# Four couples of delta heads, ScalarE statistics for three output tiles, and a smaller first constant

## The chip, the core and the metric

The kernel runs on one core of a Trainium2 chip. The core has TensorE (PE, matrix products into psum), VectorE (DVE), ScalarE (ACT), GpSimd (POOL) and SyncE (SP, which issues DMAs), each with its own queue of instructions, executed in order, and 16 DMA engines. The engines meet at semaphores. The metric is the device time of one execution in microseconds (us). The profile's span is the part of it between the first and the last recorded instruction.

## The reference

One step of a one-layer decoder, for one prompt of 512 tokens and 8 samples of 4 tokens, 544 tokens of width 1024 together:

```python
shift, scale, gate = split(silu(c) @ w_cond + b_cond)
h = x * (1 + scale) + shift
[qa, ka, va, za, qkv_b, zb, a_b, b_b, g_a, g_b] = h @ w_in     # 1024 x 11280
o_a = dilated window attention, 3 groups (128,1) (512,4) (2048,16), 8 heads x 64
o_b = gated DeltaNet, 8 heads x 128: conv of width 4, silu, l2norm, chunked delta rule
merged = sigmoid(g_a) * ((o_a * silu(za)) @ w_branch_a) + sigmoid(g_b) * ((norm(o_b) * silu(zb)) @ w_branch_b)
y = LayerNorm(ALPHA * x + gate * (merged @ w_out))
```

Beside y it returns the key and value caches (moved on by four rows), the convolution states and the delta states. The delta rule of a head treats the tokens in chunks of 64. Each chunk needs a unit lower triangular system solved:

```python
lower = where(strict, beta[:, None] * kk * decay, 0) + eye(n)
sol = triangular_solve(lower, concat([beta * v, beta * k * exp(cum)]))
```

and then the states pass from chunk to chunk. The last step, the LayerNorm over 1024 columns, needs a mean and a variance of every row.

## The kernel before

The weights of w_in come as 88 tiles of 1024 x 128. Each is loaded (wt), split by ScalarE and VectorE into a high part (hi) and the rest (lo), and multiplied with the tokens' high and low parts (hhi, hlo) in three products per 128 rows, two halves of 272 tokens each; the psum tiles are called pp. These 4080 matmuls are most of PE's work. The tiles are jobs in a list (`jobs`, from L2150), run in the list's order by `stream` (L1041): three convolution jobs (q, k, v) per delta head, nine attention jobs per pair of heads j, then za, zb and the gates. `conv_job` (L1219) of head h may begin only when head h - 3 is freed, which its `states` sets at its end, because KQ has three buffers.

Beside the stream run threads: `delta_blocks` (L1285) computes a head's decays and then the inverses of 16 x 16 blocks by substitution, fifteen pairs of VectorE instructions (tmp, then Tb) on 32 rows per head; `delta_rule` (L1389) joins the blocks to the inverse of a 64 x 64 system in six PE stages, two each at block size 16, 32 and 64 (`pd<-Tc,NTs`, `pd<-W,Xc`; `pd<-Tc,NTs`, `pd<-XF,W`; `pd<-U,NTs`, `pd<-XF,U`), with copies and transposes between them on ScalarE, VectorE and GpSimd; and `states` (L1471) carries the states through the four pairs of chunks, head after head. TOGETHER (L42) says which heads take substitution and stages in common: a couple's rows lie behind one another in the same tiles, so an instruction treats 64 rows, and a PE stage holds twice the matmuls. Before, heads 0 and 7 are alone and 1 to 6 form three couples. Other threads do the prompt's attention (`prompt_attention`), the samples' caches, and `sample_prep` (L1704), which takes the norms of the samples' queries and keys (kq: a square root on ScalarE, a reciprocal on VectorE) after head 7's convolutions.

No instruction goes to the chip as it is called. A `Recorder` keeps them with their dependencies, and its `schedule` (L459) plans the order of every engine's queue with a table of costs, by rank and readiness; `emit` (L708) issues them, at L727. Every row of the profile therefore names L727, and groups are told apart by tile names. A matmul on a part of the array (32x32, 64x64, 128x32) changes PE's form; the planner puts such a change off if it can.

The front (from L897) computes the conditioning. SP issues in order: cT, the first weights wc of part 1, bT, the constants cst, then xT, W (the 400 columns of the first projection) and wc in turn, then wc of part 0 and the first weight tiles. The constants are one table of identity, selectors (selc, selg), low16 and dmask. selc turns the conditioning rows into columns (`to_features`, L864), so it is needed at once; the identity is used by later transposes.

The end (from L2311) computes merged @ w_out by token tiles: r0 to r3 of 128 tokens by 1024 columns and r4 for the samples. VectorE scales the product by gate, adds the scaled input xr (scaled by ScalarE), takes bn_stats of each half, aggregates them to mean and variance (mv), and `norm_out` (L2332) ends with a square root on ScalarE and the normalisation on VectorE.

Of the kernel before, what the change touches and what calls it, by code (L numbers as in the profile page):

```python
# [11 lines left out]
F32 = mybir.dt.float32  # L12
# [7 lines left out]
D = 1024  # L20
# [18 lines left out]
GATES = (110.0, 200.0)  # L39
EARLY_A, EARLY_B = 7, 4  # L40
S0B = 7
TOGETHER = ((0,), (1, 2), (3, 4), (5, 6), (7,))  # L42
IDLE = (8, 2, 5)
CHUNKS = ((0, 1), (1, 1), (2, 2), (4, 2), (6, 2))

# [33 lines left out]
def shape_constants():  # L79

    p = np.arange(128)
    b4, i4, h8 = p // 32, p // 8 % 4, p % 8
    blk = {}
    blk["ident"] = np.eye(128)
    blk["selc"] = (p[:, None] % 32 == np.arange(9)[None, :])
    tok = np.arange(2 * NS)
    blk["selg"] = (p[:, None] % 32 == 1 + tok[None, :] % NS // 4)
    blk["triu"] = (p[:, None] <= p[None, :])
    same = p[:, None] // 4 == p[None, :] // 4
    blk["btri"] = same & (p[:, None] <= p[None, :])  # L90
    blk["bones"] = same
    blk["low16"] = np.where(p[:, None] % 32 >= 16, -1.0, 0.0)
    blk["strict4"] = same & (p[:, None] < p[None, :])
    blk["dmask"] = np.where(p[:, None] <= p[None, :], 0.0, -BIG)
    blk["dmask_s"] = np.where(same & (p[:, None] <= p[None, :]), 0.0, -BIG)
    blk["bmask"] = (p[:, None] % 32 // 4 == np.arange(8)[None, :])
    blk["quarter"] = np.where(p[:, None] % 32 == p[None, :] % 32, 0.25, 0.0)
    blk["hmask"] = (p[:, None] % 4 == np.arange(4)[None, :])
    sab = np.zeros((128, 4, 4))
    for h4 in range(4):  # L100
        for g in range(2):
            sab[4 * g + h4::16, h4, g] = 1.0
            sab[8 + 4 * g + h4::16, h4, 2 + g] = 1.0
    blk["selab"] = sab.reshape(128, 16)
    blk["sel16"] = p[:, None] % 16 == np.arange(16)[None, :]
    cols, blobs = {}, []
    for names in (("ident", "selc", "selg", "low16", "dmask"), ("selab", "sel16", "triu", "btri", "bones"),
                  ("strict4", "dmask_s", "bmask"), ("hmask",), ("quarter",)):
        at = 0
        for name in names:  # L110
            cols[name] = (at, blk[name].shape[1])
            at += blk[name].shape[1]
        blobs.append(np.ascontiguousarray(np.concatenate([blk[n] for n in names], axis=1), dtype=np.float32))
    return cols, blobs
# [665 lines left out]
def body(ctx, tc, io):  # L780
# [31 lines left out]
        return psp.tile([128, 512], F32, name="pp", tag="pp")  # L812


    cst = consts.tile([128, CONST[0].shape[1]], F32, name="cst")
    tables = {"early": cst}

    def take(gen, n):
        for _ in range(n):
# [44 lines left out]
    def to_features(pv, k, rows):  # L864

        for i in range(4):
            pe.matmul(pv[:, k + i, 0:9], rows[:, 128 * i:128 * i + 128], C("selc"), start=True, stop=True)

    f16 = lambda t: t[:, :128].rearrange("p (a b) -> p a b", b=16)

# [15 lines left out]
    n = CONST[1].shape[1]  # L886
# [8 lines left out]
    with ExitStack() as fctx:  # L895
# [35 lines left out]
        def cond_block(part, at, m, other):  # L931
# [18 lines left out]
            pv = ps[:, 256:256 + 16 * m].rearrange("p (a b) -> p a b", b=16)  # L950
            with rec.together():
                for i in range(m):
                    pe.matmul(pv[:, i, 0:9], Y[:, 128 * i:128 * i + 128], C("selc"), start=True, stop=True)
# [55 lines left out]
        with rec.together():  # L1009
            for t in range(4):  # L1010
                m = 128 if t < 3 else 16
                pe.matmul(pv[0:m, 16 * t:16 * t + 9], Y[:, 128 * t:128 * t + m], C("selc"), start=True, stop=True)
# [713 lines left out]

    def sample_decays(nd):

        tables["d"] = d0.tile([128, CONST[2].shape[1]], F32, name="cd")
# [393 lines left out]

    def gate_rows():

        sel = cst[:, CCOLS["selc"][0]:CCOLS["selc"][0] + 73]
        yield gates_over
        for n in range(2):
            w = slice(512 * n, 512 * n + 512)
# [184 lines left out]
    bn = [o1.tile([128, 4 if tt == 3 else 2, 6], F32, name=f"bn{tt}") for tt in range(5)]  # L2314
    parts = lambda k: ((mhi[k], 0), (mhi[k], 1), (mlo[k], 0))

    def product_out(tt, c0, c1):
# [26 lines left out]
    def samples_out():  # L2344
# [14 lines left out]
        ve.bn_stats(bn[4][:, 0, :], q)  # L2359
        mv = o2.tile([128, 4], F32, name="mv")  # L2360
        ve.bn_aggr(mv[:, 0:2], bn[4][:, 0, :])
# [13 lines left out]
    for n in range(2):  # L2375
        if n:
            samples_out()
        for tt in range(4):
            xr, q = load_x(tt, n), r[tt]
            step = 256 if tt == 3 else 512  # L2380
            for c in range(512 * n, 512 * n + 512, step):
# [4 lines left out]
                with rec.together() if at_end else nullcontext():  # L2386
                    ve.scalar_tensor_tensor(q[:, w], po, 0.5, gp[:, w], op0=OP.mult, op1=OP.mult)
                    ve.tensor_add(q[:, w], q[:, w], xr[:, c - 512 * n:c - 512 * n + step])
                    ve.bn_stats(bn[tt][:, c // step, :], q[:, w])
                    if at_end:  # L2390
                        mv = o2.tile([128, 4], F32, name="mv")
                        ve.bn_aggr(mv[:, 0:2], bn[tt].rearrange("p a b -> p (a b)"))
                rec.rank = 0
            if n:
                rec.rank = -2 * (tt == 3)
# [35 lines left out]
def lay_out(x):  # L2431
# [7 lines left out]
    d = {  # L2439
        "bias_p": bias_p,  # L2440
        "bias_s": bias_s,
        "const": CONST[0],
        "const_g": CONST[1],
        "const_d": CONST[2],
        "const_s": CONST[3],
        "const_q": CONST[4],
        "x": rows,
        "xT": rows.T.reshape(KT, 128, NT).transpose(1, 0, 2),
        "cT": c.T.reshape(KT, 128, 9).transpose(1, 0, 2),
# [59 lines left out]
```

## Time and profile before

| | |
|---|---|
| three runs | 894.52, 891.2, 893.87 us, median 893.87 |
| the profiled execution | 891.03 us |
| its span | 889.1 us, 20805 instructions |
| PE busy | 868.8 us (98%) |
| DVE, ACT, POOL busy | 646.1, 453.9, 70.0 us |
| mean DMA | 266 GB/s, 236.18 MB |

The profile is one execution. Busy time of an engine is the union of its instructions. A row of a group gives line, engine, operation, output and inputs by the program's names, form and count, then busy time and mean time of one (ns), then the idle time ahead of it and what ended that. A row of the timeline gives start, time from the first start to the last end, and the instructions. The chain of waits goes from the last instruction back to whatever released each. A wait is written "engine tile <- what it waited for: us in total, times, longest".

### The profile page before, as it was taken

The numbers are of one execution on the slowest core, as the hardware profiler recorded it, in microseconds if no ns is written. First come the engines' busy times: TensorE is split into PE (matmuls) and PEld (weight loads), VectorE is DVE, ScalarE is ACT, GpSimd is POOL, SyncE is SP. The second block draws the span as 40 slices with busy tenths as digits, with TensorE's granted clock in tenths as the row PEclk, the third lists the DMA queues.
The fourth block names the chain that finished last, engine by engine and source line by source line (L and its number), as shares of the span: only waits on it lengthen the run. The fifth ranks groups of instructions, "written<-read, shape, count | busy, mean of one in ns | idle before, by whom it ended". The sixth has DMA issues, their size and how long they took to land.

```text
span 889.1 us, 20805 instructions
## 1 busy us (share of the span) xinstructions
PE 868.8 (98%) x8212; PEld 821.2 (92%) x8212; DVE 646.1 (73%) x1338; ACT 453.9 (51%) x1083; POOL 70.0 (8%) x173
## 2 busy tenths in 40 slices
PE   8999999999999999999999998999999999999995
PEld 7899999899999999999999897999999999999884
DVE  3675447653379997489988647556999699998558
ACT  3555378844478834579734566653442222334321
POOL 0120011100001200000200100011010000001000
PEclk9999999999999999999999999999999999999998
DMA  9965785776879788888888675659969899987963
GB/s 343 337 207 178 228 281 180 237 265 197 273 218 316 242 278 297 279 274 272 272 272 263 223 231 166 199 186 281 349 228 375 275 421 403 352 306 236 355 211 120
DMA packets 106910, 236.18 MB, mean 266 GB/s; under 512 B 30407, under 2 KB 62481, under 8 KB 104125
## 3 DMA queue, kind: packets, MB, share of 16 engines
q1 hardware_dynamic: 106812, 234.86, 77.7%
q8 instruction: 64, 1.05, 0.5%
q14 instruction: 34, 0.27, 0.1%
HBM read 218.53 MB, written 103.97 MB: 363 GB/s over the span
## 4 chain that ended last, share of the span: by engine, by line
PE 89%; ACT 3%; DMA 2%; DVE 2%; SPq 1%; issue 1%; DVEq 0%; ACTq 0%
PE pp L727 68%; PE pg L727 9%; PE pd L727 8%; PE pb L727 4%; DMA wc<-in_w_cb 2%; SPq L727 1%; ACT L727 1%; DVE r L727 1%; DMA S<-in_state_delta 1%; ACT sq L727 1%; ACT hi L727 0%; DVE lo L727 0%; DVE zt L727 0%; ACT ext L727 0%; ACT acc L727 0%
## 5 line engine op out<-in xcount | busy, mean ns | idle before, releaser
L727 PE MATMUL pp<-hhi,hi 128*128 128x272 f32 x1360 | 399.8, 294 | 2.5 <-DVE spare L727 1.5
L727 PE MATMUL pp<-hlo,hi 128*128 128x272 f32 x1360 | 400.2, 294 | 0.0
L727 PE MATMUL pp<-hhi,lo 128*128 128x272 f32 x1360 | 399.2, 294 | 0.0
L727 PEld LDWEIGHTS pp<-hhi,hi 128*128 128x128 f32 x1360 | 256.3, 188 | 5.8 <-issue 1.8
L727 PEld LDWEIGHTS pp<-hhi,lo 128*128 128x128 f32 x1360 | 256.1, 188 | 3.9 <-issue 2.7
L727 PEld LDWEIGHTS pp<-hlo,hi 128*128 128x128 f32 x1360 | 256.6, 189 | 2.5 <-issue 1.5
L727 ACT ACTIVATE hi<-wt 128x1024 fp32r<-128x1024 f32 (+1 forms) x101 | 103.7, 1026 | 162.0 <-PE pp L727 137.3
L727 DVE TENSOR_TENSOR lo<-wt,hi 128x1024 fp32r<-128x1024 f32 (+1 forms) x101 | 119.0, 1179 | 80.3 <-ACT hi L727 78.6
L727 DVE SCALAR_TENSOR_TENSOR acc<-ext,cw,acc 128x568 f32<-128x568 f32 x72 | 57.8, 803 | 1.1 <-ACT acc L727 0.4
L727 ACT ACT_TABLE_LOAD x36 | 46.2, 1283 | 2.5 <-DVE acc L727 0.9
L727 DVE TENSOR_TENSOR slab<-slab 128x512 f32<-128x512 f32 (+1 forms) x66 | 43.1, 670 | 4.5 <-DMA slab<-in_ks 3.2
L727 DVE TENSOR_REDUCE slab<-slab 128x8 f32<-128x512 f32 (+2 forms) x66 | 42.9, 662 | 2.9 <-ACT slab L727 2.6
L727 ACT ACTIVATE zt<-pp 128x272 f32<-128x272 f32 x48 | 18.7, 390 | 41.0 <-PE pp L727 39.5
L727 PE MATMUL pp<-ybl,hi 128*128 128x272 f32 x128 | 37.0, 289 | 0.0
L727 PE MATMUL pp<-ybh,lo 128*128 128x272 f32 x128 | 37.0, 289 | 0.0
L727 PE MATMUL pp<-ybh,hi 128*128 128x272 f32 x128 | 36.8, 288 | 0.0
L727 ACT ACTIVATE P<-P,st 128x256 f32<-128x256 f32 (+1 forms) x64 | 31.1, 489 | 9.5 <-DVE st L727 8.8
L727 DVE CUSTOM_DVE_ANT_0 P<-pg,bias 128x256 f32<-128x256 f32 (+1 forms) x64 | 23.5, 402 | 13.0 <-PE pg L727 12.7
L727 POOL COPY cx<-ext 128x3 f32<-128x3 f32 (+1 forms) x48 | 22.2, 489 | 113.8 <-ACT ext L727 109.3
L727 ACT ACTIVATE spare<-pp 128x272 f32<-128x272 f32 (+1 forms) x32 | 16.2, 505 | 22.5 <-PE pp L727 22.4
L727 PEld LDWEIGHTS pp<-ybh,hi 128*128 128x128 f32 x128 | 24.2, 189 | 0.2
L727 PEld LDWEIGHTS pp<-ybl,hi 128*128 128x128 f32 x128 | 24.1, 188 | 0.2
(415 smaller groups left out, 1565.3 us busy)
## 6 DMA issues: line engine op xcount, KB each, us to landing
out_kv_s<-in_cache SPq DMA_DIRECT2D x144, 512.0 KB
wt<-in_w_in SPq DMA_DIRECT2D x85, 512.0 KB
out_kv_s<-in_cache SPq DMA_DIRECT2D x24, 496.0 KB
wc<-in_w_cb SPq DMA_DIRECT2D x16, 512.0 KB
slab<-in_ks SPq DMA_DIRECT2D x32, 256.0 KB
slab<-in_vs SPq DMA_DIRECT2D x32, 256.0 KB
kv<-in_ks SPq DMA_DIRECT2D x16, 512.0 KB
kv<-in_vs SPq DMA_DIRECT2D x16, 512.0 KB
```

Source lines behind the costliest of these rows:

```text
L727: getattr(real[x.engine], x.name)(*map(arg, x.args), **{k: arg(v) for k, v in x.kw.items()})
```

## The change

Three things are changed.

First, TOGETHER makes four couples (0,1), (2,3), (4,5), (6,7), and the job list is put in another order to go with it: head 1's convolutions now come between the first six and the last three attention jobs of j = 0, then those of heads 2 and 3; after j = 1 come heads 4 and 5, after j = 2 heads 6 and 7, and after j = 3 none. Before, heads 1 and 2 followed j = 0, 3 and 4 j = 1, 5 and 6 j = 2, and head 7 stood within j = 3. The planner draws up the whole order anew. Its order has 1338 - 46 = 1292 instructions on DVE and 32 instead of 36 table loads on ACT; the matmuls are the same.

On PE, ahead of the fences: pd is the psum tile of the rule, pp and pg are the projections' and attention's. A single head's first stages (head 0) before:

```order
L727 MATMUL pp<-hhi,hi 128x272
L727 MATMUL pg<-PT,vrow 64x128 x6
L727 MATMUL pd<-Tc,NTs 32x16 x16
L727 MATMUL pg<-k,q 128x256 x2
L727 MATMUL pg<-k,q 128x128 x4
L727 MATMUL pd<-W_1658,Xc 32x16 x16
```

and now those of the first couple (heads 0 and 1):

```order
L727 MATMUL pp<-hlo,hi 128x272
L727 MATMUL pd<-Tc,NTs 32x16 x32
L727 MATMUL pg<-PT,vrow 64x128 x8
L727 MATMUL pd<-W_2217,Xc 32x16 x32
L727 MATMUL pg<-k,q 128x256 x2
L727 MATMUL pg<-k,q 128x128 x4
```

Each stage holds twice the matmuls, and the attention's 64-row products (PT, vrow) have moved between the two stages of the rule.

On ACT, before, where heads 5 and 6, the attention of j = 3 (P, PT) and the samples' norms meet (kq the samples' norms, rn a head's output norm, spare here the scratch tile of a za job, sq the squares of a head's output):

```order
L727 ACTIVATE sq_7448,rn<-pd 128x128 x2
L727 ACT_TABLE_LOAD
L727 ACTIVATE kq<-pb,small 128x512
L727 ACT_TABLE_LOAD
L727 ACTIVATE spare<-pp 128x272
L727 ACT_TABLE_LOAD
L727 ACTIVATE rn<-rn 128x4
L727 ACT_TABLE_LOAD
L727 ACTIVATE spare<-pp 128x272
```

and now, on ACT where kq's root stands, within the attention jobs of j = 3:

```order
L727 ACTIVATE spare<-pp 128x272
L727 ACTIVATE spare<-pg 128x128
L727 ACT_TABLE_LOAD
L727 ACTIVATE kq<-pb,small 128x512
L727 ACTIVATE crow<-pb 81x128
L727 ACTIVATE hi<-wt 128x1024
```

and, also now on ACT, the last rn ahead of the gates (zt is a scratch tile of a zb job; ya, NB and R belong to the attention's end):

```order
L727 ACTIVATE sq_7853,rn<-pd 128x128
L727 ACTIVATE zt<-pp 128x272
L727 ACT_TABLE_LOAD
L727 ACTIVATE rn<-rn 128x4
L727 ACTIVATE ya<-pg 128x256
L727 ACTIVATE NB<-pg 128x4x32
L727 ACTIVATE R<-pg 128x512
L727 ACT_TABLE_LOAD
L727 ACTIVATE R<-R 128x256
```

The kq root has moved forward in the order, away from the states of the last heads.

Second, the statistics of r0, r1 and r2 are made by ScalarE in two passes over 1024 columns with an accumulator (the mean by a scaled copy, then the mean squares of what is left after subtracting it) in place of bn_stats on VectorE; r3 and r4 keep bn_stats. On DVE at the end, before (r_11256 is r0, r_11292 r1, r_11320 r2, r_11357 r3):

```order
L727 SCALAR_TENSOR_TENSOR r_11292<-pp,gp 128x512
L727 TENSOR_TENSOR r_11256<-r_11256,xr 128x512
L727 BN_STATS bn_11423<-r_11256 128x6
L727 TENSOR_TENSOR r_11292<-r_11292,xr 128x512
L727 BN_AGGR mv<-bn_11423 128x2
L727 BN_STATS bn_11433<-r_11292 128x6
L727 SCALAR_TENSOR_TENSOR r_11256<-r_11256,mv,lng 128x1024
L727 RECIPROCAL mv<-mv 128x1
```

and now (r_11184 is r0, r_11220 r1, r_11261 r2, r_11294 r3):

```order
L727 SCALAR_TENSOR_TENSOR r_11184<-pp,gp 128x512
L727 SCALAR_TENSOR_TENSOR r_11220<-pp,gp 128x512
L727 TENSOR_TENSOR r_11184<-r_11184,xr 128x512
L727 TENSOR_TENSOR r_11220<-r_11220,xr 128x512
L727 SCALAR_TENSOR_TENSOR r_11184<-r_11184,mv,lng 128x1024
L727 RECIPROCAL mv<-mv 128x1
L727 SCALAR_TENSOR_TENSOR r_11261<-pp,gp 128x512
```

The same place on ACT now:

```order
L727 ACTIVATE sq,mv<-r_11184 128x1024
L727 ACTIVATE mv<-mv 128x1
L727 ACTIVATE sq,mv<-r_11184,mv 128x1024
L727 ACTIVATE mv<-mv,eps_11162 128x1
L727 ACTIVATE sq,mv<-r_11220 128x1024
L727 ACTIVATE mv<-mv 128x1
L727 ACTIVATE sq,mv<-r_11220,mv 128x1024
L727 ACTIVATE xr<-xr 128x512
L727 ACTIVATE mv<-mv,eps_11162 128x1
L727 ACTIVATE xr<-xr 128x512
L727 ACTIVATE sq,mv<-r_11261 128x1024
```

VectorE's first normalisation (lng) now stands directly behind the two additions, and ScalarE's passes over a tile stand before its root.

Third, the constants are cut in two. The selectors (73 columns) are a table of their own, sel, at the place of cst on SP's queue; the rest (257 columns) comes behind the last wc and ahead of the first weight tile. The core of the diff:

```diff
-TOGETHER = ((0,), (1, 2), (3, 4), (5, 6), (7,))
+TOGETHER = ((0, 1), (2, 3), (4, 5), (6, 7))
...
-    for names in (("ident", "selc", "selg", "low16", "dmask"), ("selab", "sel16", "triu", "btri", "bones"),
+    for names in (("selc", "selg"), ("ident", "low16", "dmask"), ("selab", "sel16", "triu", "btri", "bones"),
...
-    cst = consts.tile([128, CONST[0].shape[1]], F32, name="cst")
-    tables = {"early": cst}
+    sel = consts.tile([128, CONST[0].shape[1]], F32, name="sel")
+    cst = consts.tile([128, CONST[1].shape[1]], F32, name="cst")
+    tables = {"first": sel, "early": cst}
...
                 sp.dma_start(bT, io["bT"])
-                sp.dma_start(cst, io["const"])
+                sp.dma_start(sel, io["const_f"])
             sp.dma_start(xT[:, c:c + m], io["xT"][:, c:c + m])
             sp.dma_start(W3[:, c:c + m], io["w3"][:, c:c + m])
         for c, m in two_by_two:
             load_cond(0, c, m)
+        sp.dma_start(cst, io["const"])
...
-    h = 1
     for j in range(4):
         nine = [attention_job(j, g, s) for g in range(3) for s in range(3)]
-        if j == 3:
-            jobs += nine[:6] + [conv_job(7, s) for s in (1, 0, 2)] + nine[6:]
-        else:
-            jobs += nine + [conv_job(h + i, s) for i in range(2) for s in (1, 0, 2)]
-            h += 2
+        if not j:
+            nine = nine[:6] + [conv_job(1, s) for s in (1, 0, 2)] + nine[6:]
+        jobs += nine + [conv_job(h, s) for h in (2 * j + 2, 2 * j + 3) if h < 8 for s in (1, 0, 2)]
...
         if mv is None:
-            mv = o2.tile([128, 4], F32, name="mv")
-            ve.bn_aggr(mv[:, 0:2], bn[tt].rearrange("p a b -> p (a b)"))
-        se.activation(mv[:, 2:3], mv[:, 1:2], AF.Sqrt, bias=eps5)
+            mv, sq = o2.tile([128, 4], F32, name="mv"), o1.tile([128, D], F32, name="sq")
+            se.activation(sq, q, AF.Copy, scale=1.0 / D, accum_out=mv[:, 0:1])
+            se.activation(mv[:, 3:4], mv[:, 0:1], AF.Copy, scale=-1.0)
+            se.activation(sq, q, AF.Square, bias=mv[:, 3:4], accum_out=mv[:, 1:2])
+            se.activation(mv[:, 2:3], mv[:, 1:2], AF.Sqrt, bias=eps5, scale=1.0 / D)
+        else:
+            se.activation(mv[:, 2:3], mv[:, 1:2], AF.Sqrt, bias=eps5)
         ve.scalar_tensor_tensor(q, q, mv[:, 0:1], lng, op0=OP.subtract, op1=OP.mult)
...
-                    ve.bn_stats(bn[tt][:, c // step, :], q[:, w])
+                    if tt == 3:
+                        ve.bn_stats(bn[:, c // step, :], q[:, w])
```

More of the change, by code (lines that the diff above doesn't have):

```diff
@@ L866, in to_features @@
         for i in range(4):
-            pe.matmul(pv[:, k + i, 0:9], rows[:, 128 * i:128 * i + 128], C("selc"), start=True, stop=True)
+            pe.matmul(pv[:, k + i, 0:9], rows[:, 128 * i:128 * i + 128], C("selc", "first"), start=True, stop=True)
     f16 = lambda t: t[:, :128].rearrange("p (a b) -> p a b", b=16)
@@ L885, in body @@
     early_ = op.tile([128, NT], F32, name="cg", tag="o")
-    n = CONST[1].shape[1]
+    n = CONST[2].shape[1]
     tables["g"] = early_[:, 0:n]
@@ L952, in cond_block @@
                 for i in range(m):
-                    pe.matmul(pv[:, i, 0:9], Y[:, 128 * i:128 * i + 128], C("selc"), start=True, stop=True)
+                    pe.matmul(pv[:, i, 0:9], Y[:, 128 * i:128 * i + 128], C("selc", "first"), start=True, stop=True)
                 turn_over(idle[2])
@@ L1011, in body @@
                 m = 128 if t < 3 else 16
-                pe.matmul(pv[0:m, 16 * t:16 * t + 9], Y[:, 128 * t:128 * t + m], C("selc"), start=True, stop=True)
+                pe.matmul(pv[0:m, 16 * t:16 * t + 9], Y[:, 128 * t:128 * t + m], C("selc", "first"), start=True, stop=True)
         ve.tensor_copy(shifts[:, 0:3], pv[:, 0:48].rearrange("p (a b) -> p a b", b=16)[:, :, 0:9])
@@ L1727, in sample_decays @@
     def sample_decays(nd):
-        tables["d"] = d0.tile([128, CONST[2].shape[1]], F32, name="cd")
+        tables["d"] = d0.tile([128, CONST[3].shape[1]], F32, name="cd")
         sp.dma_start(tables["d"], io["const_d"])
@@ L2124, in gate_rows @@
     def gate_rows():
-        sel = cst[:, CCOLS["selc"][0]:CCOLS["selc"][0] + 73]
         yield gates_over
@@ L2313, in body @@
     r = [o1.tile([128, D if tt < 4 else 256], F32, name=f"r{tt}") for tt in range(5)]
-    bn = [o1.tile([128, 4 if tt == 3 else 2, 6], F32, name=f"bn{tt}") for tt in range(5)]
+    bn, bns = o1.tile([128, 4, 6], F32, name="bn"), o1.tile([128, 6], F32, name="bns")
     parts = lambda k: ((mhi[k], 0), (mhi[k], 1), (mlo[k], 0))
@@ L2358, in samples_out @@
         ve.tensor_add(q, q, xr)
-        ve.bn_stats(bn[4][:, 0, :], q)
+        ve.bn_stats(bns, q)
         mv = o2.tile([128, 4], F32, name="mv")
-        ve.bn_aggr(mv[:, 0:2], bn[4][:, 0, :])
+        ve.bn_aggr(mv[:, 0:2], bns)
         pm = pd()
@@ L2388, in body @@
                     ve.tensor_add(q[:, w], q[:, w], xr[:, c - 512 * n:c - 512 * n + step])
-                    ve.bn_stats(bn[tt][:, c // step, :], q[:, w])
+                    if tt == 3:
+                        ve.bn_stats(bn[:, c // step, :], q[:, w])
                     if at_end:
                         mv = o2.tile([128, 4], F32, name="mv")
-                        ve.bn_aggr(mv[:, 0:2], bn[tt].rearrange("p a b -> p (a b)"))
+                        ve.bn_aggr(mv[:, 0:2], bn.rearrange("p a b -> p (a b)"))
                 rec.rank = 0
@@ L2441, in lay_out @@
         "bias_s": bias_s,
[L2442 to L2446, printed above, removed]
+        "const_f": CONST[0],
+        "const": CONST[1],
+        "const_g": CONST[2],
+        "const_d": CONST[3],
+        "const_s": CONST[4],
+        "const_q": CONST[5],
         "x": rows,
```

## The prediction

> **What bounds the kernel now.** I read four views in this order: the engines' busy shares and the chain that ended last (the page), busy time by stretch of the span, the waits and the chain inside the stretches where TensorE stood idle, and single rows for the prices.
>
> ```profile
> PE 868.8 (98%) x8212; PEld 821.2 (92%) x8212; DVE 646.1 (73%) x1338; ACT 453.9 (51%) x1083; POOL 70.0 (8%) x173
> PE 89%; ACT 3%; DMA 2%; DVE 2%; SPq 1%; issue 1%; DVEq 0%; ACTq 0%
> 0.00:20.00 20.00, 16.16 (x144) 13.46 (x144) 7.99 (x25) 6.50 (x12) 0.52 (x5) 1.00 0.90 334
> 400.00:500.00 100.00, 99.54 (x998) 96.28 (x997) 89.80 (x188) 60.55 (x145) 11.51 (x32) 1.00 0.84 273
> 530.00:550.00 20.00, 17.30 (x141) 15.32 (x138) 14.45 (x41) 15.28 (x37) 0.87 (x2) 1.00 0.70 216
> 870.00:889.10 19.10, 7.96 (x58) 7.34 (x56) 15.16 (x29) 1.93 (x5) 0.00 (x0) 0.83 0.35 127
> ```
>
> TensorE (PE) is busy 868.8 of 889.1 us and carries 89% of the chain. The stretches have the columns start:end, length, then PE, weight loads, VectorE (DVE), ScalarE (ACT) and GpSimd busy, PE clock, DMA share, GB/s. Of the 20.3 us in which PE is idle, 3.84 lie in the first 20 us, 2.70 between 530 and 550 and 11.14 after 870; the other 810 us hold only 2.6. So an edit counts if it takes PE work away, fills one of those three holes or opens a new one. VectorE at 73% and ScalarE at 51% can be relieved without effect, except inside the holes. The clock is full wherever PE works.
>
> **The couples: PE work.** Six PE stages of a chain (two each on 32x16, 32x32 and 64x64 blocks) serve one head or a couple. Before there are five chains, after it four with the same matmuls inside. So six stages less are entered and left. One head, then a couple:
>
> ```profile
> 568.10 0.44 PE L727 MATMUL pd<-Tc,NTs 32*32 32x16 f32 x32
> 569.54 0.44 PE L727 MATMUL pd<-W,Xc 32*32 32x16 f32 x32
> 571.95 0.44 PE L727 MATMUL pd<-Tc,NTs 32*32 32x32 f32 x16
> 576.62 0.68 PE L727 MATMUL pd<-U,NTs 64*64 64x64 f32 x8
> 227.41 0.72 PE L727 MATMUL pd<-W,Xc 32*32 32x16 f32 x64
> 230.02 0.69 PE L727 MATMUL pd<-Tc,NTs 32*32 32x32 f32 x32
> 235.68 1.14 PE L727 MATMUL pd<-U,NTs 64*64 64x64 f32 x16
> ```
>
> Two singles against one couple: 0.88 - 0.72 = 0.16, 0.88 - 0.69 = 0.19, 1.36 - 1.14 = 0.22 us, so about 0.2 us for one stage that joins another. Six of them give 1.2 us. The whole order on PE moves with them: in the programs of the two kernels, the runs of matmuls cut to less than the full 128x128 array number 72 before and 58 after, 14 less. At 0.2 us each this is 2.8 us, and I take it, because PE is the bound nearly everywhere and work that it loses there shortens the span. The lower end is the 1.2 us of the six stages alone, if the other eight, which now stand beside a run of another cut, pay at that border instead. The upper end is 0.3 us each, 4.2 us: the rows' busy times begin only when the first cut matmul starts and so hold nothing of the neighbours' delay, and a third of a microsecond is half as much again as the largest of the three differences.
>
> With two borders a run, 0.2 us are 0.1 a border. All changes of cut, those between two cut runs too, fall from 163 to 142 only; if each cost 0.1, the 21 would give 2.1 us in place of 2.8. No row here separates the two counts. [...]
>
> **The couples: other engines.** The substitution runs fifteen pairs of VectorE instructions a chain, and 64 rows cost what 32 do:
>
> ```profile
> L727 DVE TENSOR_TENSOR Tb<-Tb,tmp 64x63 f32<-64x63 f32 x6 | 1.3, 217 | 0.2
> L727 DVE TENSOR_TENSOR Tb<-Tb,tmp 32x63 f32<-32x63 f32 x4 | 0.8, 212 | 0.1
> L727 ACT ACT_TABLE_LOAD x36 | 46.2, 1283 | 2.5 <-DVE acc L727 0.9
> ```
>
> One chain less is 30 instructions of some 0.2 us, 6 us of VectorE, and the four function-table loads less that the order has (32 for 36) are 5.1 us of ScalarE. I cost both at nothing by themselves: PE's 99.5% in the stretch 400 to 500 hides them, though VectorE is at 90% there. If that cover were gone, 6 us would be the most they could return. What turns adverse is the wait: head 0 no longer starts alone but with head 1, so its buffers (three of KQ) come free later and the convolutions of head 3, and behind it 4, stand behind them; these are priced as a rival.
>
> **The knot at 533 to 546.** Here the hole in the middle of the span lies. Its waits (500 to 550) and its chain:
>
> ```profile
> PE pp L727 <- DVE spare L727: 1.5, 1, 1.5
> PE pb L727 <- ACT crow L727: 0.8, 1, 0.8
> 535.74 1.28 ACT L727
> 537.03 0.69 ACT kq L727
> 537.74 1.28 ACT L727
> ...
> 539.45 1.28 ACT L727
> 540.74 0.20 ACT rn L727
> 540.97 1.28 ACT L727
> 537.75 3.35 DVE L727 RECIPROCAL kq<-kq 128x512 f32<-128x512 f32 x1 [1.84 <-ACT kq L727]
> ```
>
> ScalarE changes its table four times in a row, because the square roots of the samples' norms (kq) and of a head's output norm (rn) alternate with the sigmoids of the gate. Attention of the last j, the chain of heads 5 and 6 and the first za tile meet there. PE runs dry of psum to write and waits 1.5 us for spare and 0.8 for crow; with the small waits it stands for the 2.70 us of the stretch. In the new order kq stands alone, among attention projections and without a state stage next to it, and the next rn has one load on each side, with halves of the first zb tiles and no kq. So the four-load row is gone. I take 2.6 us of it as gained; the adverse end is 0, if the later chain of heads 6 and 7 with attention j = 3 makes as large a hole. What is late next is VectorE, whose reciprocal of kq stays 3.35 us long but now falls where PE has projections to do.
>
> **The selectors first.** PE cannot do the front's transposing products before the constants have landed, and the weights of the first projection follow them on the same queue:
>
> ```profile
> cst<-in_const SPq DMA_DIRECT2D x1, 165.0 KB
> ACT hi L727 <- DMA W<-in_w: 8.2, 3, 4.9
> PE pb L727 <- DMA wc<-in_w_cb: 2.0, 2, 1.4
> 2.12 0.43 SPq L727 DMA_DIRECT2D cst<-in_const  x1
> 8.95 9.94 DMA wc<-in_w_cb
> L727 PE MATMUL pb<-cst,KQ x64: 270/272/330, 62.6 to 525.2; 128*128 128x128 f32 x64
> ```
>
> 165 KB ahead of xT becomes 128 x 73 x 4 bytes, 36.5 KB; 128.5 KB go behind the condition weights of both parts. At the 334 GB/s of the first stretch that is 131.6 kB / 334 = 0.39 us, and every wait on W and wc there ends on DMA (the chain has 9.94 us of it up to 18.9), so I take 0.4 us off the start. It is 0 if the compute behind each chunk, not its landing, ends last. The late table delays the first weight tiles by the same 0.4 us, hidden by PE's conditioning work; its first product with KQ comes at 62.6, some 40 us later. SP issues one transfer more, 0.43 us, but behind those that the front waits for.
>
> [...]
>
> **The statistics of three tiles.** After 870 PE is idle for 11 of 19 us and VectorE, busy for 15, decides the end. Rows of VectorE, then prices on ScalarE:
>
> ```profile
> 868.05 0.69 DVE L727 BATCH_NORM_STATS2 bn<-r 128x6 f32<-128x512 f32 x1
> ...
> 869.25 0.20 DVE L727 BATCH_NORM_AGGREGATE mv<-bn 128x2 f32<-128x12 f32 x1
> 869.38 0.69 DVE L727 BATCH_NORM_STATS2 bn<-r 128x6 f32<-128x512 f32 x1
> 869.98 1.27 DVE L727 SCALAR_TENSOR_TENSOR r<-r,mv,lng 128x1024 f32<-128x1024 f32 x1
> ...
> 884.44 1.41 DVE L727 SCALAR_TENSOR_TENSOR r<-r,mv,lnb 128x512 f32<-128x512 f32 x2
> 867.84 0.63 ACT L727 ACTIVATE xr<-xr 128x512 f32<-128x512 f32 x1 [1.18 <-DMA xr<-in_x]
> L727 ACT ACTIVATE wo1h<-wo 128x1024 fp32r<-128x1024 f32 x4 | 4.0, 1052 | 6.1 <-DMA wo<-in_w_out 5.2 <-DVE eps L727 0.9
> L727 ACT ACTIVATION_READ_ACCUMULATOR P<-P,st 128x1 f32 x64 | 12.3, 193 | 0.0
> L727 ACT ACTIVATE mv<-mv,eps 128x1 f32<-128x1 f32 x4 | 1.1, 291 | 10.2 <-DVE mv L727 10.2
> ```
>
> VectorE has hardly a gap from 868.05 to the end, 884.44 + 1.41 = 885.85. In it it loses three 128x512 statistics at 0.60 us net (869.38 to the next start, 869.98) and two aggregates of 0.13 (869.25 to 869.38): 2.1 us. The other three statistics lay before, beside its idle time. The new ScalarE chain of one tile is 1.05 + 0.19 for the mean, 0.29 to negate it, 1.05 + 0.19 for the squares and 0.29 for the root, 3.06 us. VectorE's next instruction for the tile overwrites what ScalarE reads, so it stands until the squares are done, 2.8 us after the first tile is added up, and has only the second tile's addition (0.6) to do meanwhile: about 2 us idle. The second and third tile's chains lie beside VectorE's work. So -2.1 + 2.0 is -0.1, and I take -0.2 for the start of the wait that moves with PE. From +1.0 (the scalings of xr, 0.63 us each, stand between the two chains on ScalarE and hold the third tile) to -0.9 (the first tile's halves are ready earlier, since the order puts their matmuls forward) all is possible.
>
> **The sum.** -2.8 for PE, -2.6 for the knot, -0.4 for the start, -0.2 for the tail: -6.0 us. All of it is against the profiled execution, 891.03 us, and gives 885.0. The three runs shown are 891.2, 893.87 and 894.52, so this execution is 2.8 us below their median; from the median the sum ends at 887.9. I say 887 us, 0.8% less than the median. Own bounds: -8.0 (-4.2, -2.6, -0.4, -0.9) to -0.2 (-1.2, 0, 0, +1.0). A measurement of this kernel can tell about 0.5%, 4.5 us, from no change.
>
> **The rivals.**
> - *The hole only moves* (0.25, no change). The rows for it: four heads' chains now share the attention, and between 400 and 500 VectorE is already at 90%. If the new order has as long a hole around heads 6 and 7 and only the six stages are won, -1.2 - 0.4 - 0.2 leaves 892 us from the median. Against it: the four alternating loads are not in the new order. That the statistics and the shorter substitution do nothing, since PE was never waiting for them, ends at the same place.
> - *The first couple blocks the stream* (0.13, slower). Weight jobs run in a fixed order, and the convolution of head 3 may not start before head 0's states are done. A couple's second to fifth stage, in the rows above, take from 227.41 to 236.82, 9.4 us; with 1.4 us from a first stage to a second (568.10 to 569.54) these are 10.8 us, and the last stage and the states come behind. If PE finds no other matmuls for so long, 893.9 - 6.0 + 11 gives 899. It decides from 10.5 us of new idle time on, since 6.0 are won. Against it: the first couple has head 1's projections and three attention tiles ahead of it, and PE showed no hole of this kind at any of the old couples (99.5% between 400 and 500).
> [...]
>
> **How the numbers follow.** The likeliest case has 0.62, its own range is 881 to 889 us. The lower end of the range is 893.9 - 8.0, 885.9, set from the profiled execution, 883.0, and two less for other holes of the 2.6 us between the stretches. The upper end goes through "no change" and into the slower rival, to 896, which leaves about 0.1 above. Faster 0.62, same 0.25, slower 0.13.
>
> **What would show it.** PE busy near 866 instead of 868.8; a PE idle time of 530 to 550 that is not found again anywhere between 300 and 650; ScalarE with 32 table loads and none alternating four times; W's first wait 4.5 instead of 4.9; in the tail a VectorE wait on ScalarE of about 2 us before the first tile's subtraction. A PE wait of over 5 us anywhere between 60 and 650, on a projection's psum or on a head's states, would make the prediction wrong; so would a PE busy time as before.

## The result and the profile after

The changed kernel takes 887.92 us (median of 6 runs, 885.66 to 888.99), the kernel before in the same measurement 893.07 us (6 runs, 891.2 to 894.52): a ratio of 0.9945, with a 95% interval of 0.9928 to 0.9961, some 5 us less. The prediction was 887 us. Its profiled execution took 888.47 us, span 886.7, which lies above the median of its runs, while the one of before (891.03) lies below all of its own. The two profiles differ by 2.6 us only, so half of the 5 us can't be followed in them.

The page of the changed kernel, busy times and chain:

```profile
PE 868.0 (98%) x8212; PEld 822.3 (93%) x8212; DVE 635.5 (72%) x1292; ACT 457.6 (52%) x1087; POOL 64.6 (7%) x167
PE 87%; DMA 5%; DVE 4%; ACT 2%; SPq 1%; issue 1%; DVEq 0%; ACTq 0%
```

The changed kernel by stretch of the span, with the columns of before:

```profile
0.00:20.00 20.00, 17.84 (x132) 15.30 (x136) 7.31 (x25) 6.49 (x12) 0.52 (x5) 1.00 0.91 327
400.00:500.00 100.00, 99.17 (x1034) 95.32 (x1024) 90.35 (x202) 69.40 (x193) 8.46 (x24) 1.00 0.82 271
530.00:550.00 20.00, 20.00 (x213) 17.78 (x213) 7.42 (x29) 14.43 (x46) 0.00 (x0) 1.00 0.53 168
866.00:886.70 20.70, 8.96 (x64) 8.10 (x62) 14.18 (x25) 9.10 (x21) 0.00 (x0) 0.84 0.35 128
```

The hole (a time in which PE stands idle) between 530 and 550 is filled. PE's own waits of the changed kernel, over the whole span, show where smaller ones opened:

```profile
PE pd L727 <- issue: 1.3, 1, 1.3
PE pb L727 <- DVE NTs L727: 0.8, 1, 0.8
PE pg L727 <- DMA rbo<-dO: 0.7, 1, 0.7
```

At the start PE looks busier (17.84 for 16.16), but that is no gain. The first products of the projections come later and run slowly. The first row is of the changed kernel, the second of the same products in the run that has couples and selectors only (experiment e6, with the same order up to the end):

```profile
12.12 0.82 PE L727 MATMUL pp<-x1h,hi 128*128 128x272 f32 x2
```

```profile
9.86 0.52 PE L727 MATMUL pp<-x1h,hi 128*128 128x272 f32 x2 [0.26 <-ACT x1h L727]
```

0.82 for 0.52 us and 2.3 us later: in this execution PE ran at a slower rate up to here, although the granted clock of the stretch reads 1.00. So PE's 868.0 holds slow time (17.84 us busy in the first 20, where e6 has 16.56), and the comparison of PE work below goes by the profile of e6.

### The profile page after: what moved, and what is told of

Same layout as the page of the kernel before. It is cut to its first block, busy times and chain, and to the rows that moved or that the text cites. A ratio compares the mean times of both kernels' runs of the same rounds, so it can differ in the third digit from the quotient of the medians.

```text
span 886.7 us, 20800 instructions
## 1 busy us (share of the span) xinstructions
PE 868.0 (98%) x8212; PEld 822.3 (93%) x8212; DVE 635.5 (72%) x1292; ACT 457.6 (52%) x1087; POOL 64.6 (7%) x167
## 4 chain that ended last, share of the span: by engine, by line
PE 87%; DMA 5%; DVE 4%; ACT 2%; SPq 1%; issue 1%; DVEq 0%; ACTq 0%
PE pp L727 65%; PE pg L727 10%; PE pd L727 8%; PE pb L727 4%; SPq L727 1%; DVE r L727 1%; DMA dO<-orow 1%; DMA out_kv_s<-in_cache 1%; DMA rbo<-dO 1%; DMA slab<-in_ks 1%; DVE acc L727 1%; DVE lo L727 0%; DMA wc<-in_w_cb 0%; DMA slab<-in_vs 0%; DVE slab L727 0%
## 5 line engine op out<-in xcount | busy, mean ns | idle before, releaser
L727 POOL COPY cx<-ext 128x3 f32<-128x3 f32 (+1 forms) x48 | 19.6, 436 | 140.7 <-ACT ext L727 139.2
L727 PEld LDWEIGHTS pp<-ybh,lo 128*128 128x128 f32 x128 | 24.1, 188 | 0.2
```

What stands on the lines that cost most here:

```text
L727: getattr(real[x.engine], x.name)(*map(arg, x.args), **{k: arg(v) for k, v in x.kw.items()})
```

## The experiments

Each kernel was timed beside the kernel before. The change was first taken apart into its three parts. Since the planner draws up a new order for every kernel that it is given, a "draw" below is one such order. A "cut" is the part of PE's array that a small matmul uses, and a "run" of cut matmuls is a row of them between two on the full array.

| kernel | ratio to before, 95% interval |
|---|---|
| the full change | 0.9945 (0.9928 to 0.9961) |
| e1 couples and job order | 1.0012 (0.9992 to 1.0032) |
| e2 selectors first | 1.0080 (1.0054 to 1.0106) |
| e3 ScalarE statistics | 0.9984 (0.9964 to 1.0005) |
| e4 before, planner figure moved by 10 ns | 1.0016 (0.9996 to 1.0036) |
| e5 selectors first, order of before | 1.0007 (0.9993 to 1.0020) |
| e6 couples and selectors | 0.9941 (0.9927 to 0.9955) |
| e7 full change, planner figure moved by 10 ns | 0.9982 (0.9970 to 0.9995) |
| e8 couples, rows asked for earlier | 0.9982 (0.9969 to 0.9996) |
| e9 202 full products more | 1.0305 (1.0284 to 1.0327) |
| e10 202 cut products more | 1.0698 (1.0676 to 1.0721) |
| e11 202 pairs of cut products more | 1.0967 (1.0943 to 1.0991) |
| e12 e6 with rows asked for earlier | 1.0001 (0.9987 to 1.0016) |

**e1, the couples alone.**

```diff
-TOGETHER = ((0,), (1, 2), (3, 4), (5, 6), (7,))
+TOGETHER = ((0, 1), (2, 3), (4, 5), (6, 7))
...
+        if not j:
+            nine = nine[:6] + [conv_job(1, s) for s in (1, 0, 2)] + nine[6:]
+        jobs += nine + [conv_job(h, s) for h in (2 * j + 2, 2 * j + 3) if h < 8 for s in (1, 0, 2)]
```

> The kernel before with the couples and the new job order alone; one constant table, bn_stats on VectorE for all tiles as before. Theory A (the couples' PE stages and the filled knot make the gain): the terms -2.8 and -2.6 stand here, so about 5.4 us less than before, ratio 0.994. Theory B (the gain is a matter of the order that the planner happens to draw, and the knot's filling isn't owed to the couples): this kernel's own order has 36 table loads where the full change has 32, so the knot can stand elsewhere; ratio anywhere from 0.995 to 1.003. PE's busy time falls by 2.8 us under my counting of runs, by 2.1 if each change of cut costs, by the 0.8 us that the profile of the full change shows if the borders cost less than the rows made me think.

Measured: no gain, 893.24 against 892.29 us. Its waits of PE, then its stretches, show two holes of a length that neither the kernel before nor the full change has:

```profile
PE pg L727 <- DMA rbo<-dO: 3.2, 1, 3.2
PE pg L727 <- DVE o L727: 2.8, 1, 2.8
```

```profile
610.00:620.00 10.00, 6.78 (x44) 6.59 (x44) 4.88 (x10) 2.73 (x5) 0.21 (x1) 0.85 0.90 340
800.00:810.00 10.00, 9.90 (x66) 9.68 (x67) 6.40 (x16) 3.48 (x9) 0.59 (x2) 0.83 0.48 163
```

A narrower stretch behind the first hole, of PE alone (length, PE busy, clock, DMA share, GB/s):

```profile
616.95:620.30 3.35, 3.35 (x17) 0.50 0.98 411
```

The first is a head's output that comes back from memory (rbo) too late for PE's transposes at 612, the second the samples' attention (o) at 797. Behind each the granted clock stands at 0.50 for 3.4 us, which the stretches of 10 us show as 0.85 and 0.83; that is 1.7 us of PE work lost each time. PE's busy time is 868.3 us with these 3.4 us in it, so the couples' gain is in this kernel too; two holes of 6.0 us and the clock behind them use it up.

**e2, the selectors first alone.**

```diff
-                sp.dma_start(cst, io["const"])
+                sp.dma_start(sel, io["const_f"])
...
             load_cond(0, c, m)
+        sp.dma_start(cst, io["const"])
```

> The kernel before with the selectors as a small first transfer and the other constants behind the condition weights; couples, job order and statistics as before. Theory A: 0.4 us less, ratio 0.9996, with W's first wait about 0.4 us shorter. Theory B: the planner sees other landing times and draws another order through the whole kernel, so 2 us or more either way, ratio 0.997 to 1.003. The full change's profile has 1.7 us less PE idle time in the first 20 us; if the transfer alone is the reason, this kernel shows the same 1.7 us.

Measured: 6.5 us slower (898.81), the largest move of a single part, and not near the front. A wait of PE, the row behind it and the stretches:

```profile
PE pg L727 <- issue: 3.2, 1, 3.2
```

```profile
579.75 0.61 PE L727 MATMUL pg<-cst,st 128*4 128x128 f32 x8 [3.25 <-issue]
```

```profile
570.00:580.00 10.00, 6.75 (x200) 5.87 (x199) 3.64 (x8) 3.86 (x12) 0.57 (x2) 0.96 0.49 159
580.00:590.00 10.00, 10.00 (x78) 8.96 (x71) 4.38 (x8) 3.85 (x9) 0.21 (x1) 0.53 0.01 3
```

A hole of 3.25 us is followed by 10 us at a granted clock of 0.53, which is 4.7 us of lost work: together 7.9 us. The profiled execution (901.35 us) is 10.3 us longer than that of before, so this one place makes most of it. The planner, seeing other landing times, has drawn another order, and in that one the hole arose; e5 tests whether the transfer itself has a part in it.

**e3, the statistics alone.** The diff is the third part of the change, in norm_out and where bn_stats stood.

> The kernel before with the statistics of three output tiles on ScalarE alone. Ahead of the end its order on PE is that of before but for a row, so here theory A and B agree on everything but the end. Predicted -0.2 us with bounds -0.9 to +1.0, ratio 0.9998 (0.999 to 1.001): VectorE loses 2.1 us of work on the path and waits about 2 us for ScalarE at the first tile.

Measured: 890.89 against 892.29 us, an interval that just holds 1. In its profile the hole of before at 540 is there, 1.54 and 0.83 us again; VectorE ends 7.27 us after PE's last matmul where it took 7.89 before.

**e4, another draw of the order.**

```diff
-    WAKE = {"pe": 0.06, "ve": 0.04, "se": 0.04, "ge": 0.08, "sp": 0.06}
+    WAKE = {"pe": 0.07, "ve": 0.04, "se": 0.04, "ge": 0.08, "sp": 0.06}
```

> The kernel before with one planner figure changed by 10 ns (the time that PE is reckoned to need to wake on another engine's signal, 0.06 to 0.07 us). Not one instruction is added or taken away except table loads; only the order changes, by some hundreds of rows on each engine. Theory A: the order in itself is worth little, ratio 0.999 to 1.001. Theory B: another draw of the order moves the time by some us, ratio off 1 by 0.002 or more, and the knot at 533 to 546 looks different.

Measured: 1.0016, between the two theories, with an interval that still holds 1. The profile tells more than the time does. Its stretches and its waits between 630 and 650, and ScalarE's two square roots:

```profile
500.00:550.00 50.00, 50.00 (x422) 47.75 (x421) 30.65 (x79) 32.40 (x96) 2.67 (x5) 1.00 0.55 187
640.00:650.00 10.00, 7.75 (x46) 7.08 (x45) 8.25 (x15) 4.85 (x10) 2.29 (x6) 0.83 0.86 298
```

```profile
PE pp L727 <- DVE zt L727: 1.7, 2, 1.2
PE pd L727 <- DVE ys L727: 1.0, 1, 1.0
```

```profile
533.63 0.20 ACT L727 ACTIVATE rn<-rn 128x4 f32<-128x4 f32 x1 [0.23 <-DVE rn L727]
533.84 0.69 ACT L727 ACTIVATE kq<-pb,small 128x512 f32<-128x512 f32 x1
```

The knot at 533 to 546 is filled without four couples: the roots of rn and kq stand side by side, the row of four table loads is gone, and the order has 32 loads, as the full change has. Another hole of 2.2 us, in two parts (0.98 and 1.16), stands at 641 to 644. So a draw alone moves holes of that size about.

**e5, the selectors in the order of before.** SP's one planned transfer is issued as two, so that no other engine's order changes.

```diff
+            elif hasattr(x, "cut"):
+                both = [arg(v) for v in x.args]
+                real["sp"].dma_start(*[v[:, :x.cut] for v in both])
             else:
                 getattr(real[x.engine], x.name)(*map(arg, x.args), **{k: arg(v) for k, v in x.kw.items()})
+                if hasattr(x, "rest"):
+                    real["sp"].dma_start(*[v[:, x.rest:] for v in both])
```

> The kernel before in its own order, instruction for instruction; only SP's issues differ: at the place of the 330 columns it loads 73 (the selectors, now first in the table), and the other 257 go behind the last condition weight. The planner still reckons with one transfer. This takes the redrawn order out of the 0.8% that the selectors alone lost. Theory A (the transfer itself is worth my 0.4 us): ratio 0.9995, and the first 20 us have 0.4 us less PE idle time. Theory B (a redrawn order made the loss): this kernel is no slower than before, 0.998 to 1.001. If the transfer itself does the harm, for example by its short rows or by a late table, the ratio stays near 1.008.

Measured: 1.0007, no change. The waits of the first 20 us, ScalarE's and then PE's (the lines are numbered by this kernel, three further down):

```profile
ACT hi L730 <- DMA W<-in_w: 8.1, 3, 4.3
```

```profile
PE pb L730 <- DMA wc<-in_w_cb: 1.4, 2, 1.2
PE pg L730 <- DMA wc<-in_w_cb: 1.2, 2, 0.7
```

W's longest wait is 0.6 us shorter (4.3 for 4.9), but PE still waits 2.6 us for the condition weights, where it waited 2.4. The first product with the tokens' high part (pp<-hhi,hi) starts at 40.0 us, in the profile of before at 39.9. The transfer shows no gain, though the interval would hold the forecast 0.4 us (0.9995), and the loss of e2 was the order.

**e6, couples and selectors without the statistics.**

> The full change without its third part: bn_stats on VectorE for all tiles. Its order up to the end is that of the full change. Theory A and B agree here on the size of the statistics: the one-part kernel gave -0.16%, so this one should stand 0.2 to 1.4 us above the full change, ratio to before about 0.995 to 0.997. Then couples and selectors together gain some 3 to 4 us, though the one alone gives nothing and the other loses 7: what two parts are worth can't be added up from the parts.

Measured: 886.78 us, 0.9941: the full change without the statistics is as fast as with them, where 0.2 to 1.4 us more was expected. Its order differs from the full change's only at the end. Its page and its wait:

```profile
PE 866.4 (98%) x8212; PEld 820.6 (93%) x8212; DVE 639.7 (72%) x1301; ACT 450.0 (51%) x1072; POOL 64.6 (7%) x167
```

```profile
PE pg L727 <- DMA rbo<-dO: 1.7, 2, 1.4
```

PE's work is 2.4 us less than before (868.8), and no stretch between 20 and 870 has a lowered clock. PE's last matmul ends at 873.62 instead of 877.96, 4.3 us earlier: 2.4 of work and 2.0 of idle time. The span is 3.5 us shorter (885.6 for 889.1): from VectorE's last instruction to the end it takes 4.2 us here and in the full change, 3.3 before, for which the profiles show no reason.

**e7, another draw of the full change.** The edit of e4 made in the changed kernel.

> The full change with the planner's figure for waking PE at 0.07 instead of 0.06 us; nothing else. Theory A (the change's parts carry the gain): ratio 0.994 to 0.996 as for the full change. Theory B (the drawn order carries it): anywhere from 0.992 to 1.003, and the list of PE's holes differs from that of the full change.

Measured: 0.9982, two thirds of the gain gone. PE's waits between 290 and 310 and between 790 and 810, and the stretches behind them:

```profile
PE pd L727 <- DVE z L727: 1.7, 1, 1.7
PE pg L727 <- DVE o L727: 2.0, 1, 2.0
```

```profile
300.00:310.00 10.00, 10.00 (x74) 9.75 (x74) 8.97 (x23) 6.95 (x24) 0.60 (x4) 0.83 0.82 253
800.00:810.00 10.00, 9.87 (x69) 9.64 (x68) 6.77 (x18) 3.70 (x9) 0.59 (x2) 0.87 0.57 165
```

3.7 us in two holes, and behind each 3.4 us at a clock of 0.50, 1.7 us of lost work. The profile is of the slowest of the twelve executions (893.77, the median is 890.62), so the median may hold less of this.

**e8, a hole taken away on purpose.** In the couples' kernel:

```diff
     def finish_early():
         for rows, finish in unfinished:
             rows()
-            yield 3.0
+            yield 9.0
             finish()
```

> The couples alone, with one figure changed: between asking for a head's rows and using them (the early zb tiles) 9 us of PE work in place of 3. In the couples' profile PE stood 3.2 us there for a load that took 7.2 us from issue to use, and its clock fell for some us after. If such single holes decide the time, this one goes, 3.2 us and about 1 us of the slower clock, and the ratio falls from 1.001 to about 0.997; if the chip finds the lost time elsewhere in any case (PE's work being the bound), it stays at 1.001. The other hole of the couples' order, 2.8 us at 797, may stay or move, since the planner redraws the order from here on.

Measured: 0.9982 for 1.0012, 2.7 us less, with intervals that just overlap. The wait for rbo is gone from PE's list and the one for o has fallen from 2.8 to 0.8; no stretch before 870 has a lowered clock, and PE is busy 866.3 us:

```profile
PE 866.3 (98%) x8212; PEld 820.2 (92%) x8212; DVE 640.9 (72%) x1304; ACT 454.0 (51%) x1073; POOL 65.4 (7%) x167
```

Since both holes shrank, the run does not price the one alone; it bears out that holes decided e1.

**e9 to e11, the price of a cut.** Ahead of each psum tile of the stream stands a small product more, into columns that nobody reads: on the full array, on 32x32, and on 32x32 with one on 64x64 behind it.

```diff
+                    with rec.together() if not k else nullcontext():
+                        if not k:
+                            pe.matmul(ps_[0:32, 288:320], a[0:32, 0:32], xhi(k)[0:32, 0:32], start=True, stop=True, tile_position=(0, 0))
+                        if not k:
+                            pe.matmul(ps_[0:64, 320:352], a[0:64, 0:64], xhi(k)[0:64, 0:32], start=True, stop=True, tile_position=(0, 0))
```

> The ground for the next two: the kernel before with one small product more ahead of each of 202 psum tiles of the stream (two per job), on the whole array, 32 columns, written beside the 272 columns that are read, and never used. The outputs are as before. Its order counts 75 runs of cut matmuls, 165 changes of cut. Expected: 202 x 0.03 to 0.11 us, 6 to 22 us more than before.

> The same 202 products with 32 rows and 32 weight columns only, so each cuts the array: 262 runs of cut matmuls for 75, 187 more than the kernel with the full products. By my 0.2 us a run that is 37 us more than the full products (whose own longer streaming, up to 0.1 us each, comes off); by 0.3 us, 56 us. If a run between full matmuls is nearly hidden, under 10 us.

> Each small cut product is followed by a second one on 64 rows and 64 weight columns before the full array comes back: 266 runs as in the kernel with one cut product, but 222 borders between two cut matmuls for 19, and 754 changes of cut for 543. By my count of runs (a border between two cuts costs nothing beyond its matmul) the time is that of one cut product plus 202 x some 0.01 us. By the count of changes (0.1 us each) it is 211 x 0.1 = 21 us more.

Measured: 918.37, 953.37 and 977.32 us, with 891.73 for before. The full products cost 26.6 us, more than the 22 expected, 0.13 each. PE of e9, e10 and e11:

```profile
PE 892.7 (97%) x8414; PEld 845.7 (92%) x8414; DVE 647.1 (71%) x1342; ACT 455.6 (50%) x1081; POOL 64.1 (7%) x173
```

```profile
PE 932.5 (98%) x8414; PEld 853.6 (90%) x8414; DVE 650.7 (68%) x1340; ACT 454.0 (48%) x1079; POOL 67.7 (7%) x173
```

```profile
PE 962.0 (99%) x8616; PEld 876.6 (90%) x8616; DVE 651.2 (67%) x1338; ACT 455.7 (47%) x1083; POOL 66.5 (7%) x173
```

One place each of e9, e10 and e11, in this order; the row in the middle holds the small products and the full one behind them:

```profile
305.69 0.29 PE L727 MATMUL pp<-hhi,lo 128*128 128x272 f32 x1
305.82 0.40 PE L727 MATMUL pp<-hhi,hi 128*128 128x32 f32 x2
306.05 0.28 PE L727 MATMUL pp<-hlo,hi 128*128 128x272 f32 x1
```

```profile
309.89 0.29 PE L727 MATMUL pp<-hhi,lo 128*128 128x272 f32 x1
310.11 0.52 PE L727 MATMUL pp<-hhi,hi 32*32 32x32 f32 x2
310.46 0.29 PE L727 MATMUL pp<-hlo,hi 128*128 128x272 f32 x1
```

```profile
301.08 0.28 PE L727 MATMUL pp<-hhi,lo 128*128 128x272 f32 x1
301.30 0.68 PE L727 MATMUL pp<-hhi,hi 32*32 32x32 f32 x3
301.81 0.29 PE L727 MATMUL pp<-hlo,hi 128*128 128x272 f32 x1
```

From the start of the first row to that of the third it takes 0.36, 0.57 and 0.73 us, and at most places of each kernel within 0.02 of it. Without a small product it is 0.25, as from 306.05 to 306.30 in e9. So a full product costs 0.11 there, a cut one 0.32, and the second cut one 0.16 more. The longer streaming that e10's expectation gives the full products does not show: 170 of them take 193 ns each in e9, the 170 cut ones of the same jobs 198 ns in e10.

What of this is the cut depends on what the product itself costs. e10 has 190 runs of cut matmuls more than before (262 for 72) and 380 changes of cut more (543 for 163): 61.6 us, 0.32 a run or 0.16 a change, if the product costs next to nothing, as it does inside a run (16 more of 32x32 took 0.25 us in the prediction's rows). Against e9, whose products are not cut, it has 187 runs more and takes 35.0 us more, 0.19 a run. e11 adds 211 changes, 4 runs and 202 products to e10: 24.0 us, 0.11 a change if all of it is the border between two cuts, and nothing for the border if the product costs what it does in e9. By PE's busy time it is 29.5 us or 0.14 a change, and 0.16 if the 5.1 us that e10 loses at a clock of 0.50 between 394 and 404 are taken off. So a run costs 0.19 to 0.32 us, and whether a border between two cuts costs as much as one to the full array stays open. The holes differ too (up to the last matmul PE idles 11.8 us in e9, 10.3 in e10, 4.5 in e11).

**e12, an attempt at a faster one.** e6 with the edit of e8.

> The couples and the selectors, bn_stats on VectorE, and 9 us in place of 3 between asking for the early zb rows and using them. In the profile of couples and selectors PE waited 0.33 and 1.42 us for these rows. If single holes decide, the ratio falls from 0.9941 by up to 1.75 us, to 0.992; if the redrawn later part opens another hole, it stays at 0.994 or rises.

Measured: 1.0001, the gain of e6 is gone. The wait for rbo fell to 1.0, and the later part, drawn anew, had the hole of e1 again:

```profile
PE pg L727 <- DVE o L727: 2.8, 1, 2.8
```

## Why the prediction was right

The time came out within 1 us of the forecast (887.92 for 887, where the sum from the median gave 887.9). That it is so close is in part luck: the profiles of before and e6 account for 3.5 us, the medians differ by 5.4, and what carries the largest uncertainty, the draw, was not among the terms. Of the four terms the first held in size, the second came about for another reason than given, the third shows nothing, and the fourth held in its mechanism.

**PE work, -2.8.** The size held: -2.4 us in the two profiles with couples whose PE clock was never lowered between 20 and 870 (866.4 in e6, 866.3 in e8; 868.8, 868.7 and 868.7 in before, e3 and e5). Where the clock fell for a time, taking off half of that time gives 864.9 in e1, 865.2 in e7 and 866.6 in e12, but 869.0 in e4 and 868.7 in e2, which have no four couples; these are estimates from the clock rows, and they point the same way. The way to the size is not settled. 14 runs at the 0.19 of e10 against e9 are 2.7 us, at the 0.32 of e10 against before 4.5, above the forecast's upper end; 21 changes at 0.11 to 0.16 are 2.3 to 3.4. The first and the last fit 2.4, so the measurement does not choose between the two counts. What the rows show of a cut is that the cut product of e10 took 0.21 us more than the full one of e9 in the same place (0.57 for 0.36 us).

**The knot, -2.6.** It is filled, and with the row of four table loads, as forecast: e3 and e5, which keep the order of before, keep the hole (1.54 and 0.83 to 0.85 us). But "so the four-load row is gone" was put down to the couples, and that is a matter of the draw. e4 has neither the row nor the hole without them, and e2 has no hole there either. The idle time up to PE's last matmul fell by 2.0 to 2.2 us (8.1 before, 5.9 in the full change, 6.1 in e6), since smaller holes opened elsewhere, 1.3 us on issue in the full change and 0.7 to 1.7 on rbo.

**The start, -0.4.** Nothing is to be seen of it. What did not hold is the step from "every wait on W and wc there ends on DMA" to a gain at the end of the start: in e5 ScalarE's longest wait for W is 0.6 us shorter, but PE waits as long for the condition weights, which end the stretch.

**The tail, -0.2.** The mechanism is in the profile of the changed kernel, VectorE's rows:

```profile
864.60 1.28 DVE L727 TENSOR_TENSOR r<-r,xr 128x512 f32<-128x512 f32 x2
868.01 1.29 DVE L727 SCALAR_TENSOR_TENSOR r<-r,mv,lng 128x1024 f32<-128x1024 f32 x1 [2.13 <-ACT sq L727]
...
879.74 2.74 DVE L727 SCALAR_TENSOR_TENSOR r<-r,mv,lnb 128x512 f32<-128x512 f32 x4
```

The wait was forecast as about 2 us and is 2.13. VectorE ends 7.52 us after PE (879.74 + 2.74 - 874.96), 0.37 less than before and 0.25 less than e6. In the time this can't be seen: e3 is 0.16% faster with an interval that holds 1, and the full change is no faster than e6.

**The rivals.** The first couple does not block the stream: in none of the profiles with couples has PE a hole over 0.25 us between 25 and 290, where it would lie. The rival that the hole only moves is half right. It happens in e1, e7 and e12, and without four couples in e4; the order that was drawn for the full change is one where it didn't, and one figure of 10 ns in the planner takes two thirds of the gain back. What is shown of the couples, with their job order, is 2.4 us less PE work. Their total in other draws ran from 0.9941 to 1.0012 with couples and from 1 to 1.008 without, each draw with its own holes. Whether couples make holes rarer on the whole can't be told from five draws with them and three without.

**The working.** Two slips in the prediction's figures change nothing: the stretches beside the three holes are 830 us long, not 810, and the lower bounds add up to -8.1, not -8.0.

**Left open.** The hole of 3.25 us in e2 and the one of 1.25 us at 526 in the full change are waits on "issue": no semaphore is named, and both lie inside a dense run of small products (80 in 128x4 form, 48 in 32x32 form). So do the longest such holes of e9 (2.69 us) and e10 (2.34), in 32x32 form. What held PE there is not shown.

## What to carry to other kernels

In a kernel where a planner sets the order and PE is 98% busy, an edit is worth the PE work that it removes, here 2.4 us, plus a draw of holes that can be larger than the edit (6.5 us in e2); price the work from rows, and take the draw's spread from a kernel whose order alone is redrawn. Count the runs and the changes of array cut in the whole order, not only the stages that the edit merges. When a small edit costs far more than its mechanism, look for the one hole in the stretches and at the clock behind it before blaming the edit.

## What the hardware showed beyond that

Some holes in PE's work cost more than their length: the 3.25 us of e2 came to 7.9 with the slow clock behind them. In stretches of 10 us the clock behind them reads 0.53 to 0.87, but in finer ones it is 0.50 and then 1.00 again. Behind the holes of 1.7 to 3.2 us in e1, e7 and e12 it stood at 0.50 for 3.4 us, 1.7 us of lost work each time, from about the hole's end or up to 1.4 us later. With the 3.25 us of e2 it did so for 10.2 us (PE alone, columns as in e1's narrower stretch):

```profile
579.20:589.40 10.20, 9.65 (x73) 0.50 0.01 3
589.50:592.50 3.00, 3.00 (x28) 1.00 0.95 350
```

The length of a hole alone does not decide it. Behind the 1.54 and 0.83 us of the kernel before and the 1.42 of e6 the clock stayed at 1.00, and two holes of 0.98 and 1.16 us within 3 us lowered it in e4 (at 645, 0.83 over 640 to 650) and not in e2 (at 652, 1.00 over 650 to 660). Nor do the runs show why 0.50 lasted 10.2 us in e2, with PE busy for 9.65 of them, and 3.4 us in e1, e7 and e12.

The changed kernel's profile also had a start at a slower rate, 0.82 us for two products that took 0.52 in e6 with the same order and the same granted clock of 1.00.
